# Down-product tiles of both FFNs moved to other byte places in SBUF, with a re-laid order of instructions

## The chip, the core and the metric

The kernel runs on one core of a Trainium2 chip. The metric is the time of one execution on the device, in microseconds; the median of several executions is compared, and shorter is better. One execution of the kernel before was profiled, and all rows below come from it.

## The reference

One decoder layer on 512 tokens of 1024 features, in float32:

```
h = x
h = h + 0.5 * swiglu(rmsnorm(h), ffn1 gate, up, down)        # 1024 -> 2816 -> 1024
proj = rmsnorm(h) @ w_in                                     # u, v, z, xbc, dt
ya = rmsnorm(chunked_spatial_gating(gelu(u), gelu(v)))       # chunks of 128
yb = mamba2_mixer(z, xbc, dt)                                # chunked state-space sum
h = h + concat(ya, yb) @ w_out
h = h + 0.5 * swiglu(rmsnorm(h), ffn2 gate, up, down)
h = h + sigmoid(rmsnorm(h) @ ple_gate + b) * (p @ ple_proj)
return rmsnorm(h)
swiglu(x) = (silu(x @ w_gate) * (x @ w_up)) @ w_down
```

## The kernel before, in words

Every large product is done as three matmuls of rounded parts. A float32 operand is split into a high part (rounded to TensorE's one-pass float32 form) and a low part (what the rounding left): `hi*hi + hi*lo + lo*hi`. ScalarE (ACT) makes the high part by a cast and VectorE (DVE) the low part by a subtraction. So each weight tile of 128x1024 passes through three buffers: the loaded one, its high part and its low part.

**Names.** `raw`, `rawb`, `s1` and `rawd` hold loaded weights (`rawd` those of the down product). `whi` and `wlo` are the parts of a weight tile, `whix` and `wlox` the parts of most down weights: `down` (L1113) asks for `x` at L1144, which is so for all steps but the first of the first part and three of four in the last part; these use `whi` and `wlo`. `ghi` and `glo` are the parts of g, the gated product, each 2 x 512 columns: the moving operand of the down product. `xfa` and `xfb` are the parts of the normed input of an FFN. The gate and up products run as quarter products of 24 matmuls with 256 columns; the down products have 512 columns, in banks of 6 (first part) or 12 matmuls per output tile. In the profile's names a matmul reads `output<-moving,stationary`, so `b<-ghi,whix` streams 512 columns of `ghi` past 128 columns of `whix`.

**Stages.** FFN 1 from the start to about 355 us (with the embedding product `p @ ple_proj` at its head, whose parts lie in `ghi` and `glo` too), the mixing layer to about 600 us, the product with `w_out` and the opening of FFN 2 to about 705 us, FFN 2 to 1016 us, then the gated embedding and the last norm. A down step stands between two steps of gate and up, and the last part's four down steps stand together at the end of an FFN.

**The order.** The layer is first recorded as a list of operations, cut into units (`_units`, L273: neighbouring matmuls into one output tile), and then issued in an order written out by hand as a table of unit numbers, `ORDER` (L87). Each engine runs its instructions in that order; semaphores carry the waits. SyncE (SP) issues the loads, GpSimd (POOL) those that add into a buffer.

**Byte places.** SBUF holds the constants and the shared tiles at its start (base), a left region behind them, and a right region that grows from the end. A region's tiles are laid out one behind the other in the order in which their names were first used (`Home.open`, L311). A pad may be added: in front of a left region, behind a right one (L337 to L361), in bytes per partition, from the table `PAD` (L61). All these tiles are multiples of 512 bytes long or end on one, so each region has one remainder of its places by 128. In the program as built they are:

| tiles | region | place by 128, before | place by 128, after |
|---|---|---|---|
| `raw`, `whi`, `wlo`, `tmp`, `h` | base | 0 | 0 |
| `xfa`, `xfb` (FFNs), `xa`, `xb` (mixing) | left | 64 | 64 |
| `x` (last stage) | left | 0 | 0 |
| `m`, `convin` (mixing) | right | 96 | 96 |
| `g`, `rawb`, `s1`, `p7`, `u2` (FFNs) | right | 96 | 96 |
| `ghi`, `glo`, `whix`, `wlox`, `rawd` (FFNs) | right | 96 | 0 |

Of the kernel before, what the change touches and what calls it, by code (L numbers as in the profile page):

```python
# [23 lines left out]
F32 = mybir.dt.float32  # L24
# [5 lines left out]
P = 128  # L30
# [30 lines left out]
PAD = {"sb": 0, "ffn_left": 384, "mix_left": 384, "ple_left": 448, "ffn_right": 0, "mix_right": 0, "ple_right": 0}  # L61
# [15 lines left out]
for _name, _w in _VECS:  # L77
# [211 lines left out]
def layer_kernel(ctx: ExitStack, tc: tile.TileContext, a: dict, out: bass.AP):  # L289
# [7 lines left out]
    def name_of(tag):  # L297
        count[0] += 1
        return f"{tag}_{count[0]}"
# [37 lines left out]
    def pad(pool, name):  # L337
        n = PAD[name.replace("1", "").replace("2", "")]
        if n:
# [1012 lines left out]
    dt = small("dt")  # L1352
# [651 lines left out]
```

## Time and profile before

| what | value |
|---|---|
| median of three runs | 1080.1 us (1079.7 to 1080.41) |
| profiled execution | 1079.39 us, its span 1077.7 us |
| granted TensorE clock, mean | 0.996 |
| TensorE busy | 1067.5 us (99% of the span), 7063 matmuls |
| weight loads | 962.3 us (89%) |
| VectorE, ScalarE, GpSimd busy | 803.8, 550.1, 96.6 us |

Matmuls are pipelined: a row's duration of one matmul is longer than the distance to the start of the next, so what a matmul costs a busy TensorE is read from starts in the timeline. A window's list of groups gives the mean duration in ns, by which single matmuls are told apart. "PEld" is the weight load that goes with each matmul and overlaps the matmul before it.

### The profile page before, as it was taken

How to read it: one execution, taken by the hardware profiler on the slowest of the kernel's cores; microseconds unless marked ns; L12 is line 12 of the kernel's file. 1: busy time of each engine (PE TensorE's matmuls, PEld its weight loads, DVE VectorE, ACT ScalarE, POOL GpSimd, SP SyncE). 2: the span in 40 equal slices, each digit the busy share in tenths (PEclk: the TensorE clock that was granted, in tenths of full speed). 3: DMA queues.
4: the chain of work that ended last, by engine and by line, in shares of the span. 5: the costliest groups of instructions: out<-in, count | busy, mean ns of one | idle time of the engine just before them, and what ended most of it. 6: DMA issues, size and time to landing. Idle time of an engine off the chain costs nothing.

```text
span 1077.7 us, 17409 instructions
## 1 busy us (share of the span) xinstructions
PE 1067.5 (99%) x7063; PEld 962.3 (89%) x7063; DVE 803.8 (75%) x1149; ACT 550.1 (51%) x773; POOL 96.6 (9%) x110
## 2 busy tenths in 40 slices
PE   9999999999999999999999999999999999999997
PEld 7899999999998878999999878899999999999886
DVE  6887675766677689999998666877766766766647
ACT  7645343343444537887775334455434444433536
POOL 1100000010000400000100000001000000010211
PEclk9999999999999999999999999999999999999998
DMA  9777654776631235686764334757765765544412
GB/s 330 225 191 221 189 152 163 211 161 187 172 111 59 79 120 143 167 224 163 208 150 104 98 102 152 196 117 219 197 192 137 201 188 159 175 84 143 143 45 78
DMA packets 51632, 171.16 MB, mean 159 GB/s; under 512 B 5856, under 2 KB 6112, under 8 KB 51552
## 3 DMA queue, kind: packets, MB, share of 16 engines
q1 hardware_dynamic: 34128, 117.46, 31.5%
q0 software_dynamic: 11824, 43.00, 21.9%
q10 hardware_dynamic: 5600, 9.60, 3.0%
q8 instruction: 55, 0.90, 0.3%
q14 instruction: 25, 0.20, 0.1%
HBM read 165.77 MB, written 4.26 MB: 158 GB/s over the span
## 4 chain that ended last, share of the span: by engine, by line
PE 98%; DVE 0%; ACT 0%; DMA 0%; issue 0%; DVEq 0%; SPq 0%; ACTq 0%
PE b L1896 80%; PE a L1896 18%; DMA raw<-in_ple_proj 0%; DVE o L1896 0%; ACT L1896 0%; DVE tmp L1896 0%; ACT tmp L1896 0%; DVE nt L1896 0%; ACT h L1896 0%; DVEq L1999 0%; ACT whi L1896 0%; ACT m L1896 0%; ACT ny L1896 0%; SPq L1896 0%; DVE h L1896 0%
## 5 line engine op out<-in xcount | busy, mean ns | idle before, releaser
L1896 PE MATMUL b<-xfb,whi 128*128 128x256 f32 (+1 forms) x1648 | 291.1, 280 | 0.0
L1896 PEld LDWEIGHTS b<-xfb,whi 128*128 128x128 f32 x1648 | 253.2, 188 | 6.8 <-issue 1.0
L1896 PE MATMUL b<-xfb,wlo 128*128 128x256 f32 (+1 forms) x824 | 230.7, 280 | 0.0
L1896 ACT CAST whi<-raw 128x1024 fp32r<-128x1024 f32 (+1 forms) x128 | 133.1, 1041 | 127.9 <-PE b L1896 97.3
L1896 DVE TENSOR_TENSOR wlo<-raw,whi 128x1024 fp32r<-128x1024 f32 (+1 forms) x127 | 155.2, 1228 | 51.2 <-ACT whi L1896 49.5
L1896 PEld LDWEIGHTS b<-xfb,wlo 128*128 128x128 f32 x824 | 154.7, 188 | 1.1
L1896 PE MATMUL b<-xfa,whi 128*128 128x256 f32 (+1 forms) x688 | 125.9, 285 | 0.0
L1896 PEld LDWEIGHTS b<-xfa,whi 128*128 128x128 f32 x688 | 106.4, 188 | 3.5
L1896 PE MATMUL b<-xfa,wlo 128*128 128x256 f32 (+1 forms) x344 | 98.0, 285 | 0.0
L1896 ACT CAST whix<-rawd 128x1024 fp32r<-128x1024 f32 (+1 forms) x40 | 39.5, 987 | 106.4 <-PE a L1896 58.1
L1896 ACT CAST whi<-rawb 128x1024 fp32r<-128x1024 f32 x52 | 54.5, 1049 | 63.0 <-PE b L1896 50.6
L1896 DVE TENSOR_TENSOR wlox<-rawd,whix 128x1024 fp32r<-128x1024 f32 (+1 forms) x40 | 45.6, 1140 | 43.1 <-ACT whix L1896 43.1
L1896 DVE TENSOR_TENSOR wlo<-rawb,whi 128x1024 fp32r<-128x1024 f32 x52 | 63.4, 1220 | 14.4 <-ACT whi L1896 14.2
L1896 PE MATMUL b<-m,whi 128*128 128x512 f32 x224 | 70.6, 396 | 0.0
L1896 PEld LDWEIGHTS b<-xfa,wlo 128*128 128x128 f32 x344 | 64.5, 188 | 1.1
L1896 POOL DMA_DIRECT2D raw<-in_ffn_gu x30 | 31.8, 1096 | 357.7 <-DVE wlo L1896 163.2
L1896 PE MATMUL b<-xb,whi 128*128 128x256 f32 (+1 forms) x280 | 62.2, 317 | 0.0
L1896 PE MATMUL b<-ghi,wlox 128*128 128x512 f32 x156 | 61.5, 394 | 0.0
L1896 PE MATMUL b<-glo,whix 128*128 128x512 f32 x156 | 61.3, 393 | 0.0
L1896 PE MATMUL b<-ghi,whix 128*128 128x512 f32 x156 | 60.7, 389 | 0.0
L1896 PE MATMUL a<-ghi,wlox 128*128 128x512 f32 x140 | 55.2, 394 | 0.0
L1896 PE MATMUL a<-glo,whix 128*128 128x512 f32 x140 | 54.9, 392 | 0.0
(294 smaller groups left out, 2263.2 us busy)
## 6 DMA issues: line engine op xcount, KB each, us to landing
raw<-in_ffn_gu SPq DMA_DIRECT2D x56, 512.0 KB, 5.1
rawd<-in_ffn_down SPq DMA_DIRECT2D x40, 512.0 KB, 5.0
rawb<-in_ffn_gu SPq DMA_DIRECT2D x32, 512.0 KB, 6.4
raw<-in_ffn_gu POOLq DMA_DIRECT2D x30, 512.0 KB, 7.4
s<-in_ffn_gu SPq DMA_DIRECT2D x20, 512.0 KB, 5.1
s<-in_ffn_gu POOLq DMA_DIRECT2D x20, 512.0 KB, 8.5
raw<-in_w_out SPq DMA_DIRECT2D x16, 512.0 KB, 3.9
raw<-in_w_in SPq DMA_DIRECT2D x13, 512.0 KB, 3.8
```

Of the source, the lines that this page charges most:

```text
L1896: getattr(getattr(real, engine), what)(*(real_of(x) for x in args), **{k: real_of(x) for k, x in kw.items()})
```

## The change

Two things. First, in the right region of an FFN the five names of the down product (`DOWN`) are laid out behind all others, with a gap of 416 bytes per partition in front of them, and the right region of an FFN gets a pad of 96 bytes at its end. As the region grows from the end, `DOWN` tiles start 96 bytes lower than a layout without pad would have them, and the others 512 bytes lower, which leaves their remainder by 128 (and by 512) as it was. Second, `ORDER` is another table: of the engines' instructions none is added or taken away, but many change places from the end of FFN 1 on (on DVE 925 of 1151 keep their place in a common sequence, on ACT 614 of 821, on TensorE 6642 of 6886, on SP 222 of 239).

```
+DOWN = ("whix", "wlox", "rawd", "ghi", "glo")
-PAD = {"sb": 0, "ffn_left": 384, "mix_left": 384, "ple_left": 448, "ffn_right": 0, "mix_right": 0, "ple_right": 0}
+PAD = {"sb": 0, "ffn_left": 384, "mix_left": 384, "ple_left": 448, "ffn_right": 96, "mix_right": 0, "ple_right": 0}
 ORDER = (
-    "1-2 5-7 9-10 13 11-12 3 0 14 16 18 20 24 15 17 19 25 21 26 41 27 29 42 37-38 40 39 8 43 32 34-35 33 "
+    "1-2 5-7 9-10 13 0 11-12 3 14 16 18 20 24 15 17 19 25 21 26 41 27 29 42 37-38 40 39 8 43 32 34-35 33 "
...
         def open(self, pool):
             self.pool = pool
-            for tag, (shape, dt) in self.tags.items():
+            tags = sorted(self.tags, key=lambda tag: tag in DOWN)
+            for tag in tags:
+                shape, dt = self.tags[tag]
+                if tag in DOWN and tags[tags.index(tag) - 1] not in DOWN:
+                    pool.tile([P, 104], F32, tag="gap", name=name_of("gap"))
                 n = {"b": 7, "a": 1}[tag] if self.pool is psum else BUFS.get(tag, 1)
```

Two places show what the new order moves. The first is on SP, at the opening of FFN 2 (`w_out` and `ffn_gu` loads; `s` is `s1`). Before:

```order
L1896 DMA raw_6806<-in_ffn_gu 128x1024
L1896 DMA raw_971_6496<-in_ffn_gu 128x1024
L1896 DMA raw_6809<-in_w_out 128x1024
L1896 DMA s_1043_6959<-in_ffn_gu 128x1024
L1896 DMA raw_6976<-in_ffn_gu 128x1024
L1896 DMA raw_1059_6978<-in_ffn_gu 128x1024
L1896 DMA rawb_6956<-in_ffn_gu 128x1024
L1896 DMA s_1044_6960<-in_ffn_gu 128x1024
L1896 DMA rawd_6968<-in_ffn_down 128x512
```

And in the change, the same place:

```order
L1901 DMA raw_6802<-in_ffn_gu 128x1024
L1901 DMA raw_6804<-in_w_out 128x1024
L1901 DMA rawd_6970<-in_ffn_down 128x512
L1901 DMA rawb_6955<-in_ffn_gu 128x1024
L1901 DMA rawb_6956<-in_ffn_gu 128x1024
L1901 DMA rawb_6957<-in_ffn_gu 128x1024
L1901 DMA raw_6980<-in_ffn_gu 128x1024
L1901 DMA s_1045_6958<-in_ffn_gu 128x1024
L1901 DMA s_1046_6959<-in_ffn_gu 128x1024
```

A down load and three `rawb` loads now stand ahead of the `s` loads and of the next `raw` loads, which they followed before.

The second is on TensorE, in the mixing layer, where the state-space sum's float32 matmuls (transposes with `ident`, products of `m` tiles) stand between the projections' split products. Before:

```order
L1896 MATMUL b_4285<-ident_65,m_3876 128x128
L1896 MATMUL b_4290<-m_3871,m_3864 128x128 x4
L1896 MATMUL b_4295<-m_3867,m_3865 128x128 x4
L1896 MATMUL b_4300<-xa_3523,whi_4235 128x256 x2
L1896 MATMUL b_4300<-xa_3523,wlo_4251 128x256
```

And in the change, behind a whole projection product of `xa`:

```order
L1901 MATMUL b_4292<-xa_3460,wlo_4257 128x256
L1901 MATMUL b_4317<-ident_65,m_3863 128x128
L1901 MATMUL b_4317<-ident_65,m_3869 128x128
L1901 MATMUL b_4317<-ident_65,m_3866 128x128
L1901 MATMUL b_4317<-ident_65,m_3874 128x128
L1901 MATMUL b_4353<-m_3864,m_3862 128x128 x4
L1901 MATMUL b_4358<-m_3868,m_3861 128x128 x4
L1901 MATMUL b_4363<-ident_65,m_3862 128x128 x3
L1901 MATMUL b_4367<-xb_3461,whi_4253 128x256 x2
```

The products of `m` tiles moved behind the next projection product and the next transposes. Of the whole of TensorE's order, neighbours that are one a split product and one a plain float32 matmul go from 71 to 77. The down products of FFN 1 keep their order up to the last part, and so do those of FFN 2 from its second part on.

192 rows, old and new, of the table ORDER are left out of this document.

## The prediction

> **What bounds the kernel now.** I read three views of the page first: the busy times, the shares of the chain that ended last, and the granted clock.
>
> ```profile
> PE 1067.5 (99%) x7063; PEld 962.3 (89%) x7063; DVE 803.8 (75%) x1149; ACT 550.1 (51%) x773; POOL 96.6 (9%) x110
> PE 98%; DVE 0%; ACT 0%; DMA 0%; issue 0%; DVEq 0%; SPq 0%; ACTq 0%
> core 0: 1077.7 us, clock 0.996
> ```
>
> TensorE is busy for 99% of the span and makes up 98% of the chain, at nearly full clock. So there is hardly an idle stretch to close; what can still change is the time between the starts of two matmuls, which I call the step. Does a step depend on where its operands lie? The groups by operation, shapes kept apart, set the same product side by side: 128 x 128 weights, 512 columns of `ghi` or `glo`, once with `whix` (before: both at remainder 96) and once with `whi` (96 and 0). The last columns are the busy time and the mean ns of one.
>
> ```profile
> L1896 PE MATMUL b<-ghi,whix 128*128 128x512 f32 x156 | 60.7, 389 | 0.0
> L1896 PE MATMUL b<-glo,whix 128*128 128x512 f32 x156 | 61.3, 393 | 0.0
> L1896 PE MATMUL a<-ghi,whix 128*128 128x512 f32 x140 | 54.4, 389 | 0.0
> L1896 PE MATMUL b<-glo,whi 128*128 128x512 f32 x50 | 20.0, 400 | 0.0
> L1896 PE MATMUL b<-ghi,whi 128*128 128x512 f32 x50 | 19.9, 397 | 0.7 <-ACT whi L1896 0.7
> L1896 PE MATMUL a<-ghi,whi 128*128 128x512 f32 x22 | 8.7, 395 | 0.0
> ```
>
> With equal remainders one matmul shows 389 to 393 ns, with unequal ones 395 to 400. The steps themselves stand in TensorE's timeline (start, duration). First a run of 24 products with `whix` and `wlox` and the `xfb` product behind it; then the last run of FFN 1, in its second half `whi` and `wlo` alone; then products of `x` with `whi`, both at remainder 0.
>
> ```profile
> 209.23 0.39 PE L1896 MATMUL b<-ghi,whix 128*128 128x512 f32 x1
> 211.54 0.39 PE L1896 MATMUL b<-glo,whix 128*128 128x512 f32 x1
> 214.49 0.40 PE L1896 MATMUL a<-ghi,wlox 128*128 128x512 f32 x1
> 214.72 0.28 PE L1896 MATMUL b<-xfb,whi 128*128 128x256 f32 x1
> ...
> 332.69 0.39 PE L1896 MATMUL a<-ghi,whi 128*128 128x512 f32 x1
> 343.83 0.39 PE L1896 MATMUL b<-ghi,whi 128*128 128x512 f32 x1
> 355.04 0.39 PE L1896 MATMUL b<-xa,whi 128*128 128x512 f32 x1
> ...
> 1016.01 0.63 PE L1896 MATMUL b<-x,whi 128*128 128x512 f32 x2
> 1018.09 0.61 PE L1896 MATMUL b<-x,whi 128*128 128x512 f32 x2
> 1021.49 0.39 PE L1896 MATMUL b<-x,whi 128*128 128x512 f32 x1
> ```
>
> From 209.23 to 211.54 lie 10 steps, 0.231 us each; from 211.54 to 214.49 13 steps, 0.2269 each. So equal remainders begin slowly and settle, and the settling costs 2.31 - 10 x 0.2267 = 0.043 us. At 96 and 0 the 48 steps from 343.83 to 355.04 take 0.2335 each and never settle. At 0 and 0 the first 9 steps (1016.01 to 1018.09) take 0.231 and the next 15 (to 1021.49) 0.2267: the picture of 96 and 96. I read from this that equality decides, and not the value 96.
>
> **The change, part by part.** Own time of the profiled execution: 1079.39 us, the span of 1077.7 and 1.7 around it, 0.7 below the median of the runs; differences are worked out against it and then set on the median.
>
> *Inside the runs with `whix`.* All five names move together, so `ghi` with `whix` stays equal, at 0 in place of 96. By the products of `x` above that costs the same: 0. These are 888 of the 1104 matmuls, 3 x (156 + 140). The bounds: the settling goes (56 runs begin with it, counted along the timeline: 56 x 0.043 = -2.4), or it doubles (+2.4).
>
> *The products with `whi` and `wlo`.* Those buffers stay at 0, where `ghi` and `glo` now lie too, so 3 x (50 + 22) = 216 matmuls become equal. The two runs that end the FFNs have 96 each and take 355.04 - 332.69 = 22.35 us; settled they would take 96 x 0.2267 + 0.043 = 21.81, so 2 x -0.54 = -1.08. Of the rest I show the run of 18 in FFN 2 that begins with six `whix` products:
>
> ```profile
> 725.44 0.39 PE L1896 MATMUL b<-ghi,whix 128*128 128x512 f32 x1
> 729.63 0.39 PE L1896 MATMUL b<-xfb,whi 128*128 128x256 f32 x2
> ```
>
> 4.19 us against 18 x 0.2267 + 0.043 = 4.12: -0.07. By the same rule the embedding product's two runs of 24 give -0.1 each and one run of 12 -0.04, together -0.31. Sum of this part: **-1.39**.
>
> *Where a run begins and ends.* A weight load runs under the matmul before it, so the matmul before a run streams `xfb` (64) while `whix` is loaded, and the last of a run streams `ghi` (96) while `whi` (0) is loaded. Groups of single stretches of the timeline, around 209.23 and 214.72, tell these matmuls apart from their like: the last `xfb` product before a run and the one before that; the last `ghi` product of a run and two earlier ones.
>
> ```profile
> L1896 PE MATMUL b<-xfb,wlo 128*128 128x256 f32 x1 | 0.3, 285 | 0.0
> L1896 PE MATMUL b<-xfb,wlo 128*128 128x256 f32 x1 | 0.3, 276 | 0.0
> ...
> L1896 PE MATMUL a<-ghi,wlox 128*128 128x512 f32 x1 | 0.4, 397 | 0.0
> L1896 PE MATMUL a<-ghi,wlox 128*128 128x512 f32 x1 | 0.4, 389 | 0.0
> ```
>
> The entry costs 285 - 276 = 9 ns, the exit 397 - 389 = 8. Afterwards `whix` is at 0 like `whi`, before which the timeline shows no such step, and the exit becomes a pair of 0 and 0. 56 entries x 0.009 = **-0.50**; 48 runs are long enough to settle (30 of 12 matmuls, 18 of 24) and lose 0.008 to 0.0095 at their exit: **-0.38** to -0.46. If the entry's 9 ns only moves into the settling, -0.50 falls away.
>
> *Weight parts, casts and loads.* ACT and DVE write these tiles and DMA fills `rawd`. The casts of tiles at 96 and at 0 show no price of a place:
>
> ```profile
> L1896 ACT CAST whi<-raw 128x1024 fp32r<-128x1024 f32 x126 | 131.9, 1048 | 127.0 <-PE b L1896 97.3 <-PE a L1896 8.0 <-issue 7.6
> L1896 ACT CAST whix<-rawd 128x1024 fp32r<-128x1024 f32 x34 | 35.8, 1052 | 96.5 <-PE a L1896 55.0 <-PE b L1896 39.2 <-issue 2.3
> ```
>
> 4 ns on 34 casts are 0.1 us on an engine that TensorE keeps waiting (97.3 and 55.0 us in the same rows). Cost 0; uncovered, 0.1.
>
> *The order.* Nothing is added, and what moves on DVE (75% busy), ACT (51%), SP and POOL reaches the end only where TensorE waits. The waits of its weight loads (total, times, longest) for the mixing layer and its gates are:
>
> ```profile
> PEld a L1896 <- ACT m L1896: 0.9, 2, 0.7
> PEld b L1896 <- DVE m L1896: 0.8, 1, 0.8
> PEld b L1896 <- ACT a L1896: 0.7, 1, 0.7
> PEld b L1896 <- ACT m L1896: 0.2, 1, 0.2
> PEld b L1896 <- ACT u L1896: 0.2, 1, 0.2
> ```
>
> If the products of `m`, which now stand one projection product later, find all of that ready, 2.8 us go; if the same waits come up elsewhere, nothing. TensorE changes between split products and plain float32 ones at 77 places in place of 71, three round trips more. The return from one:
>
> ```profile
> 466.68 0.51 PE L1896 MATMUL b<-xa,whi 128*128 128x256 f32 x2
> 467.14 0.39 PE L1896 MATMUL b<-xa,whi 128*128 128x256 f32 x2
> 467.48 0.39 PE L1896 MATMUL b<-xa,whi 128*128 128x256 f32 x2
> ```
>
> The first three matmuls take 0.46, the next three 0.34: 0.12 more, so 3 x 0.12 = +0.4. Between -2.8 and +0.4 and unknown new waits I take 0, since a delayed product also delays what waits for it behind `m`. What SP's new order may cost is a rival below.
>
> Sum: -1.39 - 0.50 - 0.46 = **-2.35**, say -2.4. 1079.39 - 2.4 = 1077.0 on the profiled execution, 1080.1 - 2.4 = **1077.7** on the median.
>
> **The rivals.**
>
> *The settling goes as well.* At 0 the `xf` matmul that loads the first weights no longer has its slow 9 ns, and if that jolt is what the next ten steps work off, the runs start settled: 1077.7 - 2.4 = 1075.3. For it: every run with `whix` shows jolt and settling together. Against it: the `x` products settle over nine steps too, behind unequal ones without such an entry.
>
> *The places don't matter.* The 389 against 397 ns may come from what else tells these products apart (buffers of other ages, ACT or DVE writing near them), and the change does nothing to TensorE: 1080.1. Against it: runs with `whi` stay at 0.2335 for 48 steps on end, `x` with the same `whi` at 0.2267.
> The Trainium skill (TensorE: Matmul & The Clock Gate, "Part 2: What happens when you issue a matmul") says that TensorE has two independent read ports in SBUF and that loading the next weights takes no read bandwidth from the running matmul; by this rule moving tiles changes nothing, and the time is this rival's 1080.1. The trace agrees only in part, since 0.2335 and 0.2267 differ by something that the rule does not know.
>
> *FFN 2 opens late.* SP now issues a down load and three `rawb` loads ahead of the `s` and `raw` loads. The rates (last column, GB/s) of the opening of FFN 2 and of the kernel's start, and two of ACT's casts there, which wait for TensorE to free a buffer and so show how early loads are:
>
> ```profile
> 676.00:715.00 39.00, 39.00 (x222) 33.44 (x221) 29.43 (x52) 19.38 (x28) 4.31 (x5) 1.00 0.67 163
> 0.00:60.00 60.00, 57.59 (x320) 48.86 (x321) 47.52 (x73) 40.67 (x59) 7.90 (x16) 1.00 0.86 276
> ...
> 694.45 1.05 ACT L1896 CAST whi<-raw 128x1024 fp32r<-128x1024 f32 x1 [2.71 <-PE b L1896]
> 699.89 1.05 ACT L1896 CAST whi<-raw 128x1024 fp32r<-128x1024 f32 x1 [4.38 <-PE b L1896]
> ```
>
> Four loads of 512 KB are 2.1 MB: 12.9 us at 163 GB/s, 7.6 at 276. The cover is 2.71 + 4.38 = 7.1 us, so TensorE would wait 5.8 or 0.5, and from 295 GB/s (2.1 MB in 7.1 us) on not at all. At the slow rate 1077.7 + 5.8 = 1083.5, slower than before. For it: a quarter product lasts only 24 x 0.1133 = 2.7 us (0.34 for three, above) and wants new weights behind it. Against it: 163 GB/s is what was asked for, not what could be had, and the weight loads wait for no DMA before.
>
> **How the numbers follow.** The forecast, equality gained and the order neutral, has 0.55, with its own range 1076.6 to 1078.8 (half a us either way for entries and exits, the same again for the order). The settling goes: 0.18. The places don't matter: 0.12. FFN 2 late: 0.15. The range of 8 in 10 goes from 1074.8 (the settling's case with half a us of the order's gain) to 1081.0, and leaves out most of the last case and the order's best one. About 0.2%, 2.2 us, is what a measurement tells from no change: faster means below 1077.94. Faster: 0.33 of the forecast's 0.55, which lies on that border, and 0.18 of the second, 0.51. Same: 0.22, 0.12 and 0.02, together 0.36. Slower: 0.13.
>
> **What would show it.** In the profile after, the groups of `ghi` and `glo` with `whi` fall from 395 to 400 ns to those with `whix`; the run that ends FFN 1 takes 21.8 us; the matmul before a run of `whix` shows 276 ns in place of 285 and the last of a run 389 in place of 397, while the ten steps behind the entry still take 2.31 us. The first rival is right if those ten take 2.27, the second if the `whi` groups stay at 395 to 400, the third if weight loads wait for `wlo` or a DMA between 690 and 730 us. The forecast is wrong if equal remainders at 0 step at more than 0.2267 us with `ghi`, or if the sum of the weight loads' waits moves by more than 1 us.

## The result and the profile after

The changed kernel takes 1088.05 us (median of 6, 1087.85 to 1088.57) against 1080.41 us of the kernel before in the same comparison: a ratio of 1.0071, 95% interval 1.006 to 1.0082. It is slower by 7.6 us, where 2.4 us less were forecast. The profiled execution took 1088.03 us, its span 8.6 us more than before. First the clock and the busy times of the page after:

```profile
core 0: 1086.3 us, clock 0.996
PE 1076.7 (99%) x7063; PEld 975.6 (90%) x7063; DVE 805.2 (74%) x1149; ACT 550.7 (51%) x773; POOL 98.5 (9%) x110
```

The clock is the same, TensorE is again busy 99% of the time, and its busy time grew by 9.2 us. The waits of the weight loads add up to 16.0 us before and 15.6 after. So no wait came up: the same 7063 matmuls follow each other more slowly. Which ones, the groups by operation say (shapes apart; last columns busy time, mean ns). After:

```profile
L1901 PE MATMUL b<-ghi,whix 128*128 128x512 f32 x156 | 60.8, 390 | 0.0
L1901 PE MATMUL b<-ghi,whi 128*128 128x512 f32 x50 | 19.7, 394 | 0.0
L1901 PE MATMUL a<-ghi,whi 128*128 128x512 f32 x22 | 8.6, 390 | 0.0
L1901 PE MATMUL b<-xfb,whi 128*128 128x256 f32 x1600 | 285.0, 281 | 0.0
```

and the last of them before, which the prediction did not look at:

```profile
L1896 PE MATMUL b<-xfb,whi 128*128 128x256 f32 x1600 | 275.6, 276 | 0.0
```

The down products with `whi` did fall (395 and 397 to 390 and 394). But the gate and up products, whose tiles nobody moved, rose from 276 to 281 ns, 1600 times in this group alone. The timeline of TensorE after gives the steps (start, duration): a run of 72 `xfb` and `xfa` products from 217.57, the down run behind it, and the last run of FFN 1.

```profile
217.57 0.40 PE L1901 MATMUL b<-xfb,whi 128*128 128x256 f32 x2
226.05 0.39 PE L1901 MATMUL b<-ghi,whix 128*128 128x512 f32 x1
228.32 0.39 PE L1901 MATMUL b<-glo,whix 128*128 128x512 f32 x1
...
337.41 0.39 PE L1901 MATMUL a<-ghi,whi 128*128 128x512 f32 x1
359.17 0.63 PE L1901 MATMUL b<-xa,whi 128*128 128x512 f32 x2
```

72 steps in 8.48 us are 117.8 ns each. Before, such a run stood from the row below to 209.23 (shown in the prediction): 8.17 us, 113.5 ns each.

```profile
201.06 0.39 PE L1896 MATMUL b<-xfa,whi 128*128 128x256 f32 x2
```

The down run starts settled: its first ten steps, 226.05 to 228.32, take 2.27 us in place of 2.31. The last run of FFN 1 takes 21.76 us in place of 22.35.

Added up over all starts of the timeline, the 3360 `xf` products with 256 columns went from 382.46 to 395.05 us, +12.6; the down and embedding products from 255.10 to 251.11, -4.0. Together +8.6, which is the whole difference of the spans.

The trace of before had already shown both steps, with the same tiles at the same places. One of its runs of 96 `xfb` and `xfa` products, from 269.54 to 280.67:

```profile
269.54 0.28 PE L1896 MATMUL b<-xfb,whi 128*128 128x256 f32 x1
274.98 0.43 PE L1896 MATMUL b<-xfb,whi 128*128 128x256 f32 x2
275.25 0.28 PE L1896 MATMUL b<-xfb,wlo 128*128 128x256 f32 x1
280.67 0.39 PE L1896 MATMUL b<-ghi,whix 128*128 128x512 f32 x1
```

The first 48 steps take 5.44 us, 113.3 ns each. Then two steps take 0.27 us, a hitch of 0.04. The 46 behind it take 5.42 us, 117.8 ns each, up to the end of the run. One small hitch, and the whole rest is slower; no wait in the profile goes with it. A longer hitch need not do that: in the run from 214.72, one step of 162 ns (0.05 us too long) left the matmuls behind it at 113.3. This is the theory to be tested: a stream of `xf` products has two rhythms, a fast one of 113.3 and a slow one of 117.8 ns, keeps the one that it has, and what comes right before it decides which. In the kernel before, the last `ghi` product of a settled run, during which `whi` at 0 was loaded, lasted 397 ns in place of 389 (the "exit" of the prediction); after, the group of that one matmul ahead of 217.57, and the last `xfa` matmul ahead of 226.05, read

```profile
L1901 PE MATMUL a<-ghi,wlox 128*128 128x512 f32 x1 | 0.4, 390 | 0.0
L1901 PE MATMUL b<-xfa,wlo 128*128 128x256 f32 x1 | 0.3, 282 | 0.0
```

The exit lost its 8 ns, as forecast, and with them, by this theory, what had put the next run into the fast rhythm.

### The profile page after: what moved, and what is told of

The parts are those of the page before. It is cut to its first block, busy times and chain, and to the rows that moved or that the text cites. A ratio compares the mean times of both kernels' runs of the same rounds, so it can differ in the third digit from the quotient of the medians.

```text
span 1086.3 us, 17420 instructions
## 1 busy us (share of the span) xinstructions
PE 1076.7 (99%) x7063; PEld 975.6 (90%) x7063; DVE 805.2 (74%) x1149; ACT 550.7 (51%) x773; POOL 98.5 (9%) x110
## 4 chain that ended last, share of the span: by engine, by line
PE 98%; DVE 1%; DMA 0%; ACT 0%; issue 0%; SPq 0%; DVEq 0%; ACTq 0%
PE b L1901 80%; PE a L1901 18%; DMA g<-in_p 0%; DVE o L1901 0%; ACT L1901 0%; DVE tmp L1901 0%; ACT tmp L1901 0%; DVE nt L1901 0%; ACT h L1901 0%; SPq L1901 0%; DVE glo L1901 0%; DVEq L2004 0%; ACT ghi L1901 0%; ACT m L1901 0%; ACT ny L1901 0%
## 5 line engine op out<-in xcount | busy, mean ns | idle before, releaser
L1901 PE MATMUL b<-xfb,whi 128*128 128x256 f32 (+1 forms) x1648 | 300.5, 285 | 0.0
L1901 PEld LDWEIGHTS b<-xfb,whi 128*128 128x128 f32 x1648 | 256.2, 188 | 6.4 <-issue 1.0
L1901 PE MATMUL b<-xfb,wlo 128*128 128x256 f32 (+1 forms) x824 | 234.3, 284 | 0.0
L1901 PEld LDWEIGHTS b<-xfb,wlo 128*128 128x128 f32 x824 | 158.0, 192 | 1.1
L1901 PE MATMUL b<-xfa,whi 128*128 128x256 f32 (+1 forms) x688 | 129.5, 289 | 0.0
```

The lines of the kernel that those rows point to most:

```text
L1901: getattr(getattr(real, engine), what)(*(real_of(x) for x in args), **{k: real_of(x) for k, x in kw.items()})
```

## The experiments

### The two halves of the change, each alone

`order_only` has the byte places of before, `layout_only` the `ORDER` of before:

```diff
 # order_only: kernel before
-ORDER = ( table of before )
+ORDER = ( table of the change )
 # layout_only: changed kernel
-ORDER = ( table of the change )
+ORDER = ( table of before )
```

> The new ORDER with the byte places of before. Theory of the rhythm: a matmul of xfa or xfb with 256 columns steps at 113.3 ns or at 117.8 ns, a run of them keeps the one it starts with, and the last down product before it, when it streams ghi at 96 while whi at 0 is loaded, sets the fast one; so places alone cost, the xf products stay at 113.3 to 113.8 ns and the time is 1080 +- 1.5 us. Rival, the order costs: the xf products of the FFNs take 117 to 118 ns and the time is 1086 to 1088 us.

> The new byte places with the ORDER of before. Theory of the rhythm: xf products at 117.8 ns, down products at 227 from the first matmul on, 1088 +- 1.5 us. Rival, the order costs: 1077 to 1080 us with xf products at 113.3 ns.

Measured: `order_only` 1079.76 us, ratio 0.9997 (0.9987 to 1.0006); `layout_only` 1090.76 us, ratio 1.0102 (1.0087 to 1.0117). A run of 72 `xf` products in the timeline of each:

```profile
201.17 0.28 PE L1896 MATMUL b<-xfa,whi 128*128 128x256 f32 x1
209.34 0.39 PE L1896 MATMUL b<-ghi,whix 128*128 128x512 f32 x1
```

```profile
203.76 0.40 PE L1901 MATMUL b<-xfa,whi 128*128 128x256 f32 x2
212.25 0.39 PE L1901 MATMUL b<-ghi,whix 128*128 128x512 f32 x1
```

8.17 us with the old places, 8.49 with the new ones. The places alone cost; the order alone does nothing. Yet the new places cost 10.7 us with the old order and 7.6 with the new one. Most of the difference lies at the opening of FFN 2: with the old order the weight loads wait there (680 to 735 us; total, times, longest)

```profile
PEld b L1901 <- DVE wlo L1901: 1.6, 2, 0.9
PEld b L1901 <- DVE ssum L1901: 1.4, 1, 1.4
```

for 3.0 us, and in the changed kernel, in the same stretch, only

```profile
PEld b L1901 <- issue: 0.5, 2, 0.2
```

So the new order is worth about 3 us (10.7 - 7.6 = 3.1), but only together with the new places. Why these waits come up with the new places was not followed further, and the order alone does not decide on them: `g_only` (below), which has the new order, waits 2.4 us for `ssum` in this stretch.

### Only the weights moved, and an extra matmul at the exit

In `weights_only` (order of before) `ghi` and `glo` stay at 96. `jolt64` (new places, order of before) has one more matmul between each down run and the `xf` run behind it; where the product had been begun before the down run, it starts the first 64 columns of that product anew, so those sums are changed.

```diff
 # weights_only
-DOWN = ("whix", "wlox", "rawd", "ghi", "glo")
+DOWN = ("whix", "wlox", "rawd")
 # jolt64, ahead of the first xf matmul behind a ghi or glo one
+real.tensor.matmul(ps[:, :64], w, x[:, :64], start=True, stop=True, skip_group_check=True)
```

> Order of before; only whix, wlox and rawd go to 0, ghi and glo stay at 96. Theory of the rhythm: the down products are unequal like ghi with whi before, 233.3 ns and no settling, 888 x (233.3 - 229.9) = +3.1 us; the entry's jolt of 9 ns goes (56 x 0.009 = -0.5); the exit is that of the runs with whi, behind which xf products took 113.7 ns, so they stay fast; 1080.4 + 2.6 = 1083 us. Rival, the new places slow the xf products whatever happens at the exit: 117.8 ns, +12.6 us more, 1095 us.

> The changed kernel with one more matmul (64 columns, same operands, into the bank that the next matmul starts anew) ahead of the first xf matmul behind each run of down products, some 59 in all. They cost about 0.06 to 0.12 us each, 3.5 to 7 us. Theory of the rhythm: if the extra matmul breaks the rhythm, the xf runs behind it take 113.3 ns and the time is 1088 - 12.6 + 5 = 1080 to 1081 us; if it flips only part of them, in between. Rival, the place alone sets the step: xf products stay at 117.8 ns, 1091 to 1095 us.

Measured: `weights_only` 1086.47 us (1084.67 to 1087.82), ratio 1.006 (1.0045 to 1.0075); `jolt64` 1086.73 us, ratio 1.0063 (1.0048 to 1.0078). Runs of 72 `xf` products in each, for `jolt64` without its first two matmuls:

```profile
201.84 0.40 PE L1901 MATMUL b<-xfa,whi 128*128 128x256 f32 x2
...
210.00 0.39 PE L1901 MATMUL b<-ghi,whix 128*128 128x512 f32 x1
```

```profile
203.07 0.28 PE L1915 MATMUL b<-xfa,wlo 128*128 128x256 f32 x1
211.02 0.39 PE L1915 MATMUL b<-ghi,whix 128*128 128x512 f32 x1
```

`weights_only`: 8.16 us, the fast rhythm, while its down products step at 233.3 ns throughout (888 steps, 207.17 us added up). `jolt64`: 70 steps in 7.95 us, 113.6 ns each, with every tile where `layout_only` has it. The places of `xf`, `whi` and the down tiles therefore do not set the step; what stands between the runs does. That `weights_only` missed its 1083 us has two parts: in the profiled execution (1084.67 us) the opening of FFN 2 is 2.1 us longer, as in `layout_only`; two other executions took 1087.7 and 1087.8 us at a mean clock of 0.993 in place of 0.997. An estimate from these two figures, 0.004 x 1084 = 4.3 us, is enough to cover these 3 us; they were not profiled.

### Other places for the down tiles and for xf

`down32` and `down64` keep the new order; `xf32_after` and `xf96_after` have the order of before, although their expectations call them the changed kernel, so they are `layout_only` with other places of `xf` and are compared with its 1090.76 us. The pad and the gap in front of `DOWN` add up to 512 bytes, so the other tiles stay.

```diff
 # down32: pad 64, gap 448; down64: pad 32, gap 480 bytes
-PAD = {..., "ffn_left": 384, ..., "ffn_right": 96, ...}
+PAD = {..., "ffn_left": 384, ..., "ffn_right": 64, ...}
-pool.tile([P, 104], F32, tag="gap", ...)
+pool.tile([P, 112], F32, tag="gap", ...)
 # xf32_after: layout_only with xfa, xfb at 32; xf96_after: 416 in place of 352
-PAD = {..., "ffn_left": 384, ..., "ffn_right": 96, ...}
+PAD = {..., "ffn_left": 352, ..., "ffn_right": 96, ...}
```

> The changed kernel with the five down tiles at remainder 32 in place of 0 (xf at 64, whi at 0, new order). Theory, the exit sets the rhythm: ghi at 32 streams while whi at 0 is loaded, so the exit has its jolt again as at 96, xf products are back at 113.3 to 113.8 ns, down products settle again (229.9), about 1080 us. Rival, 96 alone is special: xf products at 117.8 ns, 1086 to 1088 us.

> The down tiles at remainder 64, where xf lies. Theory, the exit sets the rhythm: at the exit ghi at 64 streams while whi at 0 is loaded, the pair at which xf runs at 113.3, so xf products are fast; the entry loads whix at 64 under xf at 64: if that is a jolt like the one to 96, 1080 us, if not, the down runs start without it, 1077 to 1079.5. Rival, only 96 drives the xf products into the fast rhythm: 117.8 ns, 1086 to 1088 us.

> The changed kernel with the FFNs' left region (xfa, xfb) at remainder 32 in place of 64; down tiles at 0. Theory, the rhythm is a phase between streams and weight loads, kept from run to run, and no exit jolt comes: the xf products take one step throughout the FFNs, either 117.8 ns (1088 us) or, if at 32 the phase of the settled down products is a free one, 113.3 ns (1088 - 12.6 = 1075.5). Rival, the place of the xf tiles alone sets their step, as for ghi with whi: a third value, above 117.8, and more than 1090 us.

> As the one before with xfa and xfb at remainder 96, where ghi with whi at 0 stepped at 233.3 for 512 columns before. Theory of the phase: one step throughout, 117.8 (1088) or 113.3 ns (1075.5); rival, place alone: 120 ns as for x with whi (half of 233.3 is 116.7), 1085 to 1095 us.

| down tiles / xf | median us | ratio (95%) |
|---|---|---|
| 32 / 64 | 1079.83 | 1.0002 (0.9993 to 1.0011) |
| 64 / 64 | 1089.15 | 1.0086 (1.0069 to 1.0102) |
| 0 / 32 | 1096.08 | 1.0148 (1.0133 to 1.0163) |
| 0 / 96 | 1095.76 | 1.0146 (1.0131 to 1.0161) |

For `down32` and then `down64`: the group of the last `ghi` matmul of a run, and the first and next row around a run of 72 `xf` products.

```profile
L1901 PE MATMUL a<-ghi,wlox 128*128 128x512 f32 x1 | 0.4, 396 | 0.0
...
201.74 0.40 PE L1901 MATMUL b<-xfa,whi 128*128 128x256 f32 x2
209.92 0.39 PE L1901 MATMUL b<-ghi,whix 128*128 128x512 f32 x1
```

```profile
L1901 PE MATMUL a<-ghi,wlox 128*128 128x512 f32 x1 | 0.4, 388 | 0.0
...
218.25 0.28 PE L1901 MATMUL b<-xfb,whi 128*128 128x256 f32 x1
226.73 0.39 PE L1901 MATMUL b<-ghi,whix 128*128 128x512 f32 x1
```

At 32 the exit is long (396 ns) and the run is fast (8.18 us); at 64 the exit is short (388) and the run slow (8.48). With 96 (397, fast) and 0 (390, slow) all four remainders agree: a settled run hands over the fast rhythm where its exit is long. The rival that 96 alone is special falls, and so does my picture that at 64 the pair of `xf` would carry over.

The runs of 72 with `xf` at 32 and at 96:

```profile
219.42 0.28 PE L1901 MATMUL b<-xfb,whi 128*128 128x256 f32 x1
227.96 0.39 PE L1901 MATMUL b<-ghi,whix 128*128 128x512 f32 x1
```

```profile
219.31 0.40 PE L1901 MATMUL b<-xfb,whi 128*128 128x256 f32 x2
227.83 0.40 PE L1901 MATMUL b<-ghi,whix 128*128 128x512 f32 x1
```

8.54 and 8.52 us, 118.6 and 118.3 ns. Both are one step throughout, but a third value, which the rival of the place had foreseen and the theory of the phase not. So place does matter here too, by half a nanosecond to one; whether this is the slow rhythm with something on top or a third rhythm was not tested. Added up over all starts, against `layout_only` the `xf` products take 4.1 us more at 32 and 3.1 at 96, the down products 0.8 and 2.5. The opening of FFN 2 is 2.6 us longer than in the changed kernel, as in `layout_only`, which has the same order; it does not come from the place of `xf`.

### Extra matmuls that change no sum, and only g moved

The extra matmul now streams 8 or 64 columns of a tile of zeros, at the exits (`zero8`, `zero64`) or ahead of the 25th `xf` matmul of a run (`mid8`). `g_only` leaves the weights' parts at 96. All have the new order.

```diff
 # zero8, zero64, mid8
+zeros = constant("zeros", (P, P), F32R)
+real.tensor.matmul(ps[:, :JOLT], w, zeros[:, :JOLT], start=start, stop=False, skip_group_check=True)
 # g_only
-DOWN = ("whix", "wlox", "rawd", "ghi", "glo")
+DOWN = ("ghi", "glo")
```

> The changed kernel with one more matmul of 8 columns at each of 58 exits from down to xf products; its moving operand is a tile of zeros (a constant of 512 bytes that leaves all remainders as they are), so the sums stay as they are. Theory of the lasting rhythm: a short jolt flips it like the one of 64 columns, which cost 29 ns and 111 ns in the steps behind it; with 8 columns 40 to 100 ns, so xf products at 113.3, down products settling a little (227.6): 1088.05 - 12.6 + 0.8 + 58 x 0.07 = 1080.3, 1078.5 to 1082 us. Rival, only a long break (the 64 columns took 204 ns with the step behind) flips it: 117.8 ns, 1089 to 1092 us.

> The same with 64 columns. Theory of the lasting rhythm: as with 64 columns of xf before, 140 ns at each exit, xf products at 113.3 behind it: 1088.05 - 12.6 + 0.8 + 58 x 0.14 = 1084.4, 1083 to 1086 us. Rival, it was the moving operand's place (xf) in the extra matmul that flipped it, which the zeros (another place) don't: 1090 to 1097 us.

> The changed kernel with the 8-column matmul of zeros not at the exit but ahead of the 25th xf matmul of each run, 42 in all. Theory of the lasting rhythm: the first 24 of each run stay at 117.8 ns, those behind the extra matmul take 113.3, with all tiles where they are; some 1500 of 2830 slow xf matmuls are faster by 4.45 ns, -6.7 us, + 42 x 0.07 = +3: 1084 us, 1082 to 1086. Rival, places and the exit set the step for the whole run: 117.8 on both sides of the extra matmul, 1090 to 1093 us.

> The changed kernel with only ghi and glo at 0; whix, wlox, rawd back at 96. The down products with whix are unequal (0 and 96): 233.3 ns, 888 x 6.6 = +5.9 us against the changed kernel. The exit is that of the changed kernel, ghi at 0 with whi at 0, without a jolt. Theory A, the settled run moves the phase and the jolt at the exit only moves it back: an unequal run never settles, xf products stay at 113.3: 1088 - 12.6 + 5.9 = 1081 us. Theory B, the pair at the exit decides alone: xf at 117.8 ns, 1094 us.

Measured: `zero8` 1096.34 us (three executions; a fourth took 6134.85 us, which is not explained), 1.0155 (1.0138 to 1.0172); `zero64` 1084.32, 1.0044 (1.0029 to 1.0059); `mid8` 1093.86, 1.0128 (1.0111 to 1.0145); `g_only` 1092.26, 1.0114 (1.0099 to 1.013). The same run of 72 in `zero8` and in `zero64`, without its first two matmuls:

```profile
206.75 0.28 PE L1917 MATMUL b<-xfa,wlo 128*128 128x256 f32 x1
215.00 0.40 PE L1917 MATMUL b<-ghi,whix 128*128 128x512 f32 x1
```

```profile
203.35 0.28 PE L1917 MATMUL b<-xfa,wlo 128*128 128x256 f32 x1
211.30 0.39 PE L1917 MATMUL b<-ghi,whix 128*128 128x512 f32 x1
```

70 steps in 8.25 us (117.9 ns) and in 7.95 (113.6). So a disturbance as such is not enough. Around it both look alike: the extra matmul starts 0.03 us ahead of the first `xf` one, and the two skipped steps take 0.32 us together. In `mid8` the run from 157.21, with the extra matmul at 160.03, stays slow on both sides of it:

```profile
157.21 0.28 PE L1917 MATMUL b<-xfb,whi 128*128 128x256 f32 x1
160.03 0.17 PE L1902 MATMUL b<-zeros,whi 128*128 128x8 f32 x1
160.38 0.28 PE L1917 MATMUL b<-xfb,wlo 128*128 128x256 f32 x1
165.80 0.40 PE L1917 MATMUL b<-ghi,whix 128*128 128x512 f32 x1
```

(24 steps in 2.82 us; 46 in 5.42, 117.8.) After `zero8` this no longer speaks against the rhythm; it only shows again that 8 columns don't flip it. `g_only` decided between neither of its theories: a run of 96 behind 24 down products, then one of 48 behind 12, each below the group of its exit:

```profile
L1901 PE MATMUL a<-ghi,wlox 128*128 128x512 f32 x1 | 0.4, 396 | 0.0
...
187.78 0.28 PE L1901 MATMUL b<-xfb,whi 128*128 128x256 f32 x1
198.70 0.39 PE L1901 MATMUL b<-ghi,whix 128*128 128x512 f32 x1
...
L1901 PE MATMUL a<-ghi,wlox 128*128 128x512 f32 x1 | 0.4, 393 | 0.0
...
248.59 0.28 PE L1901 MATMUL b<-xfb,whi 128*128 128x256 f32 x1
254.24 0.39 PE L1901 MATMUL a<-ghi,whix 128*128 128x512 f32 x1
```

96 steps in 10.92 us (113.75 ns), 48 in 5.65 (117.7): with the same places and the same pair at the exit, the run behind 24 down products is fast and the one behind 12 slow. So it is throughout: the 18 runs behind 24 `whix` products (exit 396 ns) reach the fast step, the 36 behind 6 or 12 (exit 393 to 394) are slow. Neither the pair of places nor the length of the exit alone decides, since in `weights_only` an exit of 394 ns was followed by steps of 113.3 ns. What seems to count is where in its beat the unequal down run ends.

### Four more lengths

`zero16`, `zero32`, `zero48`, `zero128` differ from `zero8` in the number of columns alone.

```diff
-JOLT = 8
+JOLT = 16   # 32, 48, 128
```

> The zeros matmul at the exits with 16 columns. With 8 the runs stayed at 117.8 ns, with 64 they flipped to 113.3, though both take 28 ns and 200 ns with the step behind. Theory of a threshold, a longer extra stream shifts the weight load behind it far enough from some length on: 16 is near 8, xf at 117.8, 1095 to 1098 us. Theory of a phase that returns, slow and fast alternate with the number of columns: fast here or at 32, 1083 to 1086 us.

> With 32 columns. Threshold: either side, 117.8 (1096) or 113.3 ns (1084.5). Phase that returns: slow if 16 was fast, fast if 16 was slow.

> With 48 columns. Threshold: fast, 113.3 ns, 1084.5 us, and fast at every greater length. Phase that returns: slow here although 64 is fast (1096 us) is possible.

> With 128 columns; some 0.03 to 0.1 us more at each of 58 exits than with 64. Threshold: fast, 113.3 ns, 1086 to 1090 us. Phase that returns: slow is possible, 117.8 ns, 1098 to 1102 us.

One execution each: 1096.86, 1096.41, 1084.09 and 1096.37 us. A run of 72 (without the first two) of `zero32`, `zero48` and `zero128`:

```profile
206.61 0.28 PE L1917 MATMUL b<-xfa,wlo 128*128 128x256 f32 x1
214.85 0.40 PE L1917 MATMUL b<-ghi,whix 128*128 128x512 f32 x1
```

```profile
230.89 0.28 PE L1917 MATMUL b<-xfb,wlo 128*128 128x256 f32 x1
238.83 0.39 PE L1917 MATMUL b<-ghi,whix 128*128 128x512 f32 x1
```

```profile
220.87 0.28 PE L1917 MATMUL b<-xfb,wlo 128*128 128x256 f32 x1
229.11 0.40 PE L1917 MATMUL b<-ghi,whix 128*128 128x512 f32 x1
```

8, 16 and 32 columns (8.24 us for 70 steps at 32, the same at 16) leave the slow rhythm, 48 (7.94 us) and 64 give the fast one, 128 (8.24 us) the slow one again. In each of the four traces all 56 runs behind an exit with steps of about 0.1 us agree. No threshold does that; a phase that returns fits.

No version beat both kernels. The two rhythms' best halves, down runs that start settled and fast `xf` runs, come together nearly in `zero48` and `zero64`. But in `zero64` each extra matmul costs 0.03 us of its own, 0.09 more in the first `xf` step (0.20 in place of 0.113) and 0.016 in the next three, 0.13 us, while the down runs gain only 255.10 - 253.29 = 1.8 us over 58 exits, 0.03 each, against the kernel before. In `zero48` they gain 255.10 - 251.78 = 3.3 us, 0.06 each, which is still less than the price.

## Why the prediction was wrong

- **The products with `whi` and `wlo`** (-1.39): right. The runs of 96 take 21.76 us where 21.81 was worked out; all 216 together 50.98 to 49.81, -1.2.
- **Inside the runs with `whix`** (0): wrong, by the rival. The settling went (2.27 us for ten steps), and with the exits the 888 products gained 204.12 - 201.30 = 2.8 us. The reason given for that rival (no jolt at the entry) fits; the `x` products, held against it, were entered out of an unequal run.
- **Where a run begins and ends** (-0.50 and -0.46): this is the step that failed. "Afterwards ... the exit becomes a pair of 0 and 0" was right as a place: the exit fell from 397 to 390 ns. But I priced the two matmuls at the border and nothing behind them. The exit's 8 ns went with the fast rhythm of the 24 to 168 `xf` products that follow: without it 3360 products cost 12.6 us more. This term was put at -0.46 and brought +12.6 behind the border. The entry's 9 ns did not go as reckoned either: the last `xfa` product takes 282 ns, like every `xf` product now.
- **Weight parts, casts and loads** (0): right as far as the page shows (ACT 550.7 us busy, DVE 805.2).
- **The order** (0): right for the old places (0.9997). With the new places the new order saves some 3 us of waits at the opening of FFN 2.
- **FFN 2 late**: did not happen; the loads that SP issues in another order kept nobody waiting. The slower case that I gave was the wrong mechanism.
- **The places don't matter**: fell as well. By the rule of the Trainium skill (TensorE: Matmul & The Clock Gate, "Part 2: What happens when you issue a matmul"), that loading the next weights takes no read bandwidth from the running matmul, as the prediction read it, moving tiles should have changed nothing. The runs disagree with that reading: one and the same product steps at 113.3 or 117.8 ns. Whether the two reads are what meets here no row shows.

The deeper mistake: I took a step of 113.3 ns as a property of the pair (64, 0), because the mean over its group hid the other value. The rows from 269.54 to 280.67 stood in the trace of before and contradict it.

What is shown: the two rhythms, that a run keeps its own unless a hitch breaks in, and that the border before the run selects it. That this is a phase between the moving stream and the weight loads is argued from the six lengths and from `g_only`; no row of the profile shows the loads' reads. Why a long exit of a settled run goes with the fast rhythm stays open.

## What to carry to other kernels

When matmuls follow each other without a gap, look at the steps in the order of time and not only at group means: if one product has two steps, its speed depends on what came before, and no edit at that border can be priced by the border alone. A small cost at a border (here 8 ns) may go with the speed of the run behind it; before removing it, find out in the trace what a run does that lacks it. Two operands' places are worth trying as a whole layout on the chip, since single pairs of places do not add up.

## What the runs showed of the hardware

- `xf` products of 256 columns with 128 x 128 weights, in float32's rounded form, step at 113.3 or at 117.8 ns with the same operands at the same places, and keep their rhythm for up to 168 matmuls. A hitch of 0.04 us changed it once, one of 0.05 us did not.
- Which of the two a run gets turned with the length of one matmul ahead of it: 8, 16, 32 columns slow, 48, 64 fast, 128 slow.
- With equal remainders of down tiles, 0 and 64 gave a short exit and `xf` steps of 117.8 ns, 32 and 96 a long exit and steps of 113.3 ns.
- The extra matmul of 8 columns moved the next start by only 0.03 us, but the step behind it took 0.20 us in place of 0.113, as did that of 64. With 128 columns it was 0.057 and 0.171. For all six lengths the two steps add up to 0.228 to 0.230 us, so the short matmul cost about as much as one more step.
